# Five pairs of split weight buffers instead of four in a macaron trunk kernel, with silu, gate product and final norm done in place and the convolution's input projection wholly in split weights

## The chip, the cores and the metric

One core of one Trainium2 chip runs the whole program. The metric is the device time of one execution in microseconds (us). TensorE (PE) does the matmuls, VectorE (DVE) and ScalarE (ACT) the elementwise work, GpSimd (POOL) a few additions, and SyncE (SP) issues the weight transfers.

## The reference, cut to what matters

A trunk of two layers on x of 256 rows and 1024 columns, all in float32. Every layer adds half a gated feed-forward block, a mixer, and half a second feed-forward block. The mixer of layer 0 is a pair of convolutions, that of layer 1 is attention.

```
def swiglu_ffn(x, w_gate_up, w_down):
    gate, up = jnp.split(x @ w_gate_up, 2, axis=-1)
    return (jax.nn.silu(gate) * up) @ w_down

def conv_mixers(h, w_in, a_kernel, b_kernel, b_bias, b_ln_g, b_ln_b, w_out):
    z = h @ w_in
    a_b, a_c, a_x, b_val, b_gate = jnp.split(z, [...], axis=-1)
    y_a = a_b * causal_depthwise_conv(a_c * a_x, a_kernel)
    u = b_val * jax.nn.sigmoid(b_gate)
    u = causal_depthwise_conv(u, b_kernel) + b_bias.astype(u.dtype)
    y_b = jax.nn.silu(layer_norm(u, b_ln_g, b_ln_b))
    return jnp.concatenate([y_a, y_b], axis=-1) @ w_out

for layer in range(DEPTH):
    x = x + 0.5 * swiglu_ffn(rms_norm(x, ffn1_norm[layer]), ...)
    x = x + mixer(rms_norm(x, mix_norm[layer]))
    x = x + 0.5 * swiglu_ffn(rms_norm(x, ffn2_norm[layer]), ...)
return rms_norm(x, final_norm)
```

`D_FF` is 2816; `a_kernel` has 3 taps and `b_kernel` 31, on 512 channels each.

## The kernel before, in words

**Layout.** x lies in SBUF as eight tiles of 128 columns by 256 rows (`x[:, 0]` to `x[:, 7]`). The gain of a norm is put on x before a projection and the factor r of each row after it (`twice(r)`), so that a projection may start before r is known.

**Weights.** The weights come as a stream of units of 1 MB, each 128 by 2048 numbers or 16 tiles of 128 by 128, in the order of use. `load` (L111) brings a unit into one of four `raw` buffers. `split` (L117) makes two parts from it: ACT rounds it into `w1` (L126), DVE subtracts, `w2 = raw - w1` (L127), each in halves of 128x1024, or in quarters for the units in `FINE`. There are `WS` = 4 pairs of `w1` and `w2`. A raw buffer comes free when its unit has been split, a pair when PE has used it. `advance(u, n)` (L130) asks for loads up to unit `u + RAWS + WS - 1` and for splits up to `u + n`; the program calls it once per unit. Units in `whole` are not split: PE reads them from their raw buffer.

**Matmuls.** With a split unit and a split operand, `mm2` (L166) does two matmuls for each weight tile, one of 512 columns (L168) and one of 256 (L169). `mm3` (L158) does three of 256 columns (L162 to L164), and for a whole unit a single float32 one (L160), which the trace records as two.

**Stages.** Feed-forward (`ffn`, L364): 22 units for gate and up (p from 0 to 21) fill PSUM banks of the tag `pa`, of which there are four. `project2` (L324) takes two banks for a p, `project` (L314) one; the first stage takes one for p of 1 to 3 and also for the first p, whose unit is whole (L352). `join` (L334) or a product (L381) makes v from the banks, ACT makes the silu (L385), DVE the gate product (L387), and `split_to` (L183) splits the product. Then 22 units for down (L392), whose sums DVE adds to x (L404) tile by tile; with each tile `after.add` splits the next stage's operand (`xs`, L189 and L190) and sums its squares.

**Convolution stage** (`conv`, L422). Its 14 units are counted from `first_conv`: 0 to 9 for ten projections (p), 10 to 13 for the output projection. `WHOLE` names those that stay whole: 2 and 9, whose operand is `xg` (L428, eight activations), and 10 to 13. Projections 0 to 3 give u (L498 to L500), 4 to 7 give the short convolution `ya` (L513 to L522), 8 and 9 its gate (L532, L533). The 31 taps are shared: DVE does some (L463, sums in PSUM), while ACT makes products (`prod`, L485, 18 buffers) that POOL adds one after the other into `yp` (L486, 55 additions). L472 joins the two in y. Then the output projection on `ya` (`out_half`, first half) runs while the layer norm of y is worked out (L555 to L571); its result `ob` feeds the second half, and DVE adds the sums to x (L419). `AHEAD[p]` is how far `advance` may split at projection p, `PER_STEP` and `PER_POOL` how many taps are put behind it.

**What sets the order.** Each engine runs its instructions in program order. That order is set by a scheduler, from the order of the code, `tc.high_priority` and the `advance` calls; a wait on one engine holds all that stands behind it there.

Of the kernel before, what the change touches and what calls it, by code (L numbers as in the profile page):

```python
# [10 lines left out]
F32 = mybir.dt.float32  # L11
F32R = mybir.dt.float32r
I32 = mybir.dt.int32
AF = mybir.ActivationFunctionType
# [3 lines left out]
P = 128  # L18
D = 1024
S = 256  # L20
DEPTH = 2
FF = 2816
ND = D // P
# [10 lines left out]
UT = 16  # L34
# [2 lines left out]
POOL_TAPS = [13, 17, 13, 16]  # L37
PER_STEP = [9, 8, 7, 8, 8, 8, 9, 8, 9, 10]
PRIO = 0
WHOLE = {2, 9, 10, 11, 12, 13}  # L40
PBUFS = 18
PER_POOL = [6, 8, 2, 6, 6, 9, 6, 4, 8, 9]
XPRIO = 0
AHEAD = [2, 4, 1, 1, 4, 4, 3, 4, 3, 3]
LATE = 15
OUT_AHEAD = [2, 3]
PRIO_LN = 800
# [18 lines left out]
M_POOL = [0, 0, 0, 0]  # L66
B_POOL = [0, 0]
RAWS = 4
WS = 4
TWO = (3,)  # L70
ROBIN = False
SU_POOL = 2
# [21 lines left out]
def trunk(ctx: ExitStack, tc: tile.TileContext, xin, wst, cst, bia, idn, out):  # L94
    nc = tc.nc
# [5 lines left out]
    tmp = ctx.enter_context(tc.tile_pool(name="tmp", bufs=2))  # L101
# [70 lines left out]
    x = keep.tile([P, ND, S], F32, name="x")  # L172
    xs_all = keep.tile([P, ND * 2 * S + LINE // 4], F32R, name="xs")
    const_all = keep.tile([P, LINE // 4], F32, name="const")
    const = const_all[:, :NCONST]
# [17 lines left out]
    def rsqrt_of(sums, n, eps, eps_tile=None):  # L193

        ts = [slice(t, t + 1) for t in range(2)]
        with tc.high_priority(offset=0 if eps_tile is not None else PRIO_C):
            pt = psb.tile([P, 2, 2], F32, name="pb")
            for i, part in enumerate(sums):
                for t in range(2):
                    nc.tensor.matmul(pt[:, t, :], part[:, t * P:(t + 1) * P], ones[:, :2],  # L200
                                     start=i == 0 and t == 0, stop=i == len(sums) - 1,
                                     skip_group_check=True)
            a = tmp.tile([P, 2], F32, name="ra")
            y = tmp.tile([P, 2], F32, name="ry")
            q = tmp.tile([P, 2], F32, name="rq")
            if eps_tile is None:
                for t, c in enumerate(ts):
                    nc.vector.tensor_scalar(q[:, c], pt[:, t, :1], 1.0 / n, eps,
                                            op0=ALU.mult, op1=ALU.add)
                for c in ts:  # L210
                    nc.vector.tensor_scalar(y[:, c].bitcast(I32), q[:, c].bitcast(I32), 1, None,
                                            op0=ALU.logical_shift_right)
                for t, c in enumerate(ts):
                    nc.vector.tensor_scalar(a[:, c], pt[:, t, :1], -0.5 / n, -0.5 * eps,
                                            op0=ALU.mult, op1=ALU.add)
                for c in ts:
                    nc.vector.tensor_scalar(y[:, c].bitcast(I32), y[:, c].bitcast(I32), -1,
                                            0x5F3759DF, op0=ALU.mult, op1=ALU.add)
            else:
                nc.scalar.activation(y, pt[:, :, 0], AF.Sqrt, scale=1.0 / n, bias=eps_tile)  # L220
                nc.vector.tensor_scalar(a, pt[:, :, 0], -0.5 / n, -0.5 * eps,
                                        op0=ALU.mult, op1=ALU.add)
                for c in ts:
                    nc.vector.reciprocal(y[:, c], y[:, c])
            n = 3 if eps_tile is None else 1
            for i in range(n):
                for c in ts:
                    nc.vector.scalar_tensor_tensor(q[:, c], y[:, c], a[:, c], y[:, c],
                                                   op0=ALU.mult, op1=ALU.mult)
                for c in ts:  # L230
                    nc.vector.scalar_tensor_tensor(q[:, c] if i == n - 1 else y[:, c], q[:, c],
                                                   0.5 if i == n - 1 else 1.5, y[:, c],
                                                   op0=ALU.add, op1=ALU.mult)
            for c in ts:
                nc.vector.tensor_add(y[:, c], y[:, c], q[:, c])
            wide = tmp.tile([P, 2, P], F32, name="wide")
            pr = psb.tile([P, S], F32, name="pb")
            for t, c in enumerate(ts):
                nc.vector.tensor_copy(wide[:, t], y[:, c].to_broadcast([P, P]))
                nc.tensor.matmul(pr[:, t * P:(t + 1) * P], wide[:, t], ident,  # L240
                                 start=True, stop=True)
        return y, pr
# [68 lines left out]
    def twice(r):  # L311
        return r[:, None, :].to_broadcast([P, 2, S])

    def project(st, base, xs, xg=None):  # L314

        bank = psa.tile([P, 2, S], F32, name="pa")
        for i in range(2):
            for k in range(ND):
                w = st.tile(base + 2 * k + i)
                b = (xs[:, k, 0], xs[:, k, 1]) if len(w) == 2 else (xg[:, k],)  # L320
                mm3(bank[:, i], w, b, k == 0, k == ND - 1)
        return bank

    def project2(st, base, xs):  # L324
# [39 lines left out]
    def ffn(norm, after, between=None, first=None):  # L364
        _, r = norm.end(True, first is None)
        with tc.tile_pool(name="gp", bufs=1, reuse_waits="tile") as gp:
            st = take(NF)
# [3 lines left out]
            for p in range(NF):  # L371
                advance(st.u + p)
                one = p < ONES[st.u // FFN_STEP] or p >= NF - ONE_END
                if one:
                    bank = first if first and p == 0 else project(st, p * UT, norm.xs)
                else:
                    banks = project2(st, p * UT, norm.xs)
                with tc.high_priority(offset=PRIO_F):
                    v = tmp.tile([P, 2, S], F32, name="v")
                    if one:  # L380
                        nc.vector.tensor_mul(v, bank, twice(r))  # L381
                    else:
                        join(v, banks, r)
                    sl = tmp.tile([P, S], F32, name="sl")
                    nc.scalar.activation(sl, v[:, 0], AF.Silu)  # L385
                    g = tmp.tile([P, S], F32, name="g")
                    nc.vector.tensor_mul(g, sl, v[:, 1])  # L387
                    split_to(gs[:, p, 0], gs[:, p, 1], g)
            if between:
                between(gs[:, NF - 1, 0, :1].bitcast(F32))  # L390
            st = take(NF * ND // UT)
# [30 lines left out]
    def conv(norm, after):  # L422
        with tc.tile_pool(name="cp", bufs=1, reuse_waits="tile") as cp, \
                tc.tile_pool(name="cp2", bufs=PBUFS, reuse_waits="tile") as cp2:
            xg = cp.tile([P, ND, S], F32, name="xg")
            with tc.high_priority(offset=XPRIO):
                for k in range(ND):
                    nc.scalar.activation(xg[:, k], x[:, k], AF.Copy,  # L428
                                         scale=const[:, norm.col + k:norm.col + k + 1])
            _, r = norm.end(WIDEC)  # L430
            ob = cp.tile([P, 4, S], F32, name="ob")
            u = cp.tile([P, 4, KB - 1 + S], F32, name="u")
# [57 lines left out]
            st = take(10)  # L490
            for p in range(10):
                advance(st.u + p, AHEAD[p])
                bank = project(st, p * UT, norm.xs, xg)
                c = p % 4
                with tc.high_priority(offset=PRIO):
                    if p < 4:
# [6 lines left out]
                        queue_v += new[:LATE] + [f for f in [held_last] if f] + new[LATE:]  # L503
                        queue_p += [(c, f) for f in taps_p(c)]
                    elif p < 8:
                        t = tmp.tile([P, S], F32, name="g")
                        mc = m[:, c, KA - 1:]
                        if M_POOL[c]:
                            nc.scalar.copy(t, bank[:, 0])
# [211 lines left out]
            ffn(norm, nxt)  # L721
            norm = nxt
    with tc.tile_pool(name="fp", bufs=1, reuse_waits="tile") as fp:
        y = fp.tile([P, ND, S], F32, name="y")
        eps = fp.tile([P, 1], F32, name="eps")
        warm = fp.tile([P, 1], F32, name="warm")
        nc.vector.memset(eps, RMS_EPS)
# [98 lines left out]
```

## Time and profile before

| | |
|---|---|
| median of 3 runs | 960.96 us (960.74 to 962.14) |
| the profiled execution | 960.66 us, span 958.9 us |
| granted TensorE clock | 0.997 of full speed |
| PE busy | 945.5 us, 99% of the span |
| DVE busy | 724.3 us, 76% |
| ACT busy | 543.3 us, 57% |
| POOL busy | 47.1 us, 5% |
| mean DMA rate | 184 GB/s |

All times in the rows are counted from the start of the span. "Busy" for PE is from the start of a matmul to its modelled end, and matmuls overlap; the pace is therefore read from starts. "Idle before" in a row is the engine's idle time just before it, and the arrow names what ended it. The 2.1 us between the execution and its span lie around the program.

### The profile page before, as it was taken

Reading aid. Unit: us, or ns where it says so; the run is one execution under the profiler, and the core shown is the slowest. Engines: PE = TensorE matmul, PEld = TensorE weight load, DVE = VectorE, ACT = ScalarE, POOL = GpSimd, SP = SyncE. Lnnn points to the kernel's source line nnn. Section 1 sums busy time; section 2 is a strip of 40 time slices with the busy share of each in tenths; the row PEclk is TensorE's granted clock in tenths of the full one; section 3 lists DMA queues with packets and bytes.
Section 4 is the critical chain, followed back from the end, with each engine's and each line's share of the span. In section 5 each row is a group of like instructions: output and inputs, shape, how many; then the busy total and the mean of one; then the engine's idle time right before and its main releaser. Section 6 shows DMA issues by size and latency. Waiting matters only on the chain.

```text
span 958.9 us, 15090 instructions
## 1 busy us (share of the span) xinstructions
PE 945.5 (99%) x5828; PEld 845.8 (88%) x5828; DVE 724.3 (76%) x1373; ACT 543.3 (57%) x975; POOL 47.1 (5%) x61
## 2 busy tenths in 40 slices
PE   8999999999999999999999999999999999999996
PEld 7988898999888888988988889898888998889886
DVE  7988866688879878766788877665698798788552
ACT  6666554488265565554466565444676565665541
POOL 0000000049600000000000000000000000000000
PEclk9999999999999999999999999999999999999998
DMA  8855555544176555555455555555553455555501
GB/s 328 291 205 192 178 206 189 178 159 148 45 260 213 193 207 181 180 211 181 176 194 202 176 191 205 178 195 212 195 191 129 149 186 194 194 202 177 194 26 44
DMA packets 27287, 176.24 MB, mean 184 GB/s; under 512 B 3024, under 2 KB 3792, under 8 KB 6864
## 3 DMA queue, kind: packets, MB, share of 16 engines
q1 hardware_dynamic: 26784, 174.67, 51.7%
q8 instruction: 45, 0.74, 0.3%
q10 hardware_dynamic: 432, 0.63, 0.2%
q14 instruction: 26, 0.21, 0.1%
HBM read 174.23 MB, written 1.05 MB: 183 GB/s over the span
## 4 chain that ended last, share of the span: by engine, by line
PE 90%; POOL 3%; DVE 3%; ACT 1%; DMA 1%; issue 1%; SPq 0%; DVEq 0%; POOLq 0%; ACTq 0%
PE pa L168 33%; PE pa L169 17%; PE pb L168 15%; PE pb L169 8%; PE pa L162 4%; PE pa L163 3%; PE pa L164 3%; POOL yp L486 3%; PE pa L160 2%; PE pb L162 1%; PE pb L163 1%; PE pb L164 1%; DVE pb L463 1%; PE pa L352 1%; PE pb L652 1%
## 5 line engine op out<-in xcount | busy, mean ns | idle before, releaser
L127 DVE TENSOR_TENSOR w<-raw,w 128x1024 fp32r<-128x1024 f32 (+1 forms) x316 | 377.0, 1205 | 136.3 <-ACT w L126 135.9
L168 PE MATMUL pa<-xs,w 128*128 128x512 f32 x1376 | 479.4, 391 | 0.1
L126 ACT CAST w<-raw 128x1024 fp32r<-128x1024 f32 (+1 forms) x316 | 320.5, 1032 | 133.5 <-PE pa L168 49.7
L169 PE MATMUL pa<-xs,w 128*128 128x256 f32 x1376 | 387.2, 282 | 0.0
L168 PEld LDWEIGHTS pa<-xs,w 128*128 128x128 f32 x1376 | 258.1, 188 | 54.9 <-DVE xs L190 0.7
L169 PEld LDWEIGHTS pa<-xs,w 128*128 128x128 f32 x1376 | 260.0, 189 | 0.3
L168 PE MATMUL pb<-gs,w 128*128 128x512 f32 x616 | 213.7, 390 | 0.0
L169 PE MATMUL pb<-gs,w 128*128 128x256 f32 x616 | 173.7, 282 | 0.0
L168 PEld LDWEIGHTS pb<-gs,w 128*128 128x128 f32 x616 | 115.6, 188 | 24.1
L169 PEld LDWEIGHTS pb<-gs,w 128*128 128x128 f32 x616 | 116.4, 189 | 0.0
L385 ACT ACTIVATE sl<-v 128x256 f32<-128x256 f32 x88 | 36.8, 418 | 108.7 <-DVE v L340 104.3
L338 ACT COPY sq<-pa 128x256 f32<-128x256 f32 x172 | 62.9, 366 | 28.6 <-PE pa L169 26.1
L163 PE MATMUL pa<-xs,w 128*128 128x256 f32 x272 | 76.3, 281 | 0.1
L162 PE MATMUL pa<-xs,w 128*128 128x256 f32 x272 | 76.3, 282 | 0.0
L164 PE MATMUL pa<-xs,w 128*128 128x256 f32 x272 | 76.2, 281 | 0.0
L339 DVE TENSOR_TENSOR v<-pa,sq 128x256 f32<-128x256 f32 x156 | 65.5, 420 | 0.0
L404 DVE SCALAR_TENSOR_TENSOR x<-pb,x 128x256 f32<-128x256 f32 x60 | 25.4, 423 | 42.5 <-PE pb L169 28.5
L189 ACT ACTIVATE xs<-x,const 128x256 fp32r<-128x256 f32 x48 | 24.3, 506 | 55.2 <-DVE x L404 43.1
L486 POOL TENSOR_TENSOR yp<-yp,prod 128x256 f32<-128x256 f32 x55 | 45.1, 822 | 208.8 <-ACT prod L485 204.8
L340 DVE TENSOR_TENSOR v<-v,rr 128x512 f32<-128x512 f32 x78 | 53.6, 688 | 0.0
L162 PEld LDWEIGHTS pa<-xs,w 128*128 128x128 f32 x272 | 51.4, 190 | 0.3
L163 PEld LDWEIGHTS pa<-xs,w 128*128 128x128 f32 x272 | 51.1, 188 | 0.5 <-DVE xs L190 0.3
(155 smaller groups left out, 900.7 us busy)
## 6 DMA issues: line engine op xcount, KB each, us to landing
raw<-wst SPq DMA_DIRECT2D x159, 1024.0 KB, 4.8
bt<-bia SPq DMA_DIRECT2D x8, 384.0 KB, 3.3
raw<-wst SPq DMA_DIRECT2D x7, 256.0 KB, 6.3
raw<-wst SPq DMA_DIRECT2D x2, 512.0 KB, 5.6
x<-xin SPq DMA_DIRECT2D x3, 256.0 KB, 5.7
out<-y SPq DMA_DIRECT2D x2, 256.0 KB, 2.5
out<-y ACTq DMA_DIRECT2D x2, 256.0 KB, 2.4
x<-xin SPq DMA_DIRECT2D x2, 128.0 KB, 3.2
```

The source lines that it names most:

```text
L126: nc.scalar.copy(w1[u][:, c], raw[u][:, c])
L127: nc.vector.tensor_sub(w2[u][:, c], raw[u][:, c], w1[u][:, c].bitcast(F32))
L162: nc.tensor.matmul(o, a[0], b[0], start=start, stop=False, skip_group_check=check)
L163: nc.tensor.matmul(o, a[0], b[1], start=False, stop=False, skip_group_check=check)
L164: nc.tensor.matmul(o, a[1], b[0], start=False, stop=stop, skip_group_check=check)
L168: nc.tensor.matmul(o, w[0], b, start=start, stop=False, skip_group_check=True)
L169: nc.tensor.matmul(o[:, 0], w[1], b[:, 0], start=False, stop=stop, skip_group_check=True)
L338: nc.scalar.copy(h, bank[:, 1])
L339: nc.vector.tensor_add(v[:, i], bank[:, 0], h)
L340: nc.vector.tensor_mul(v, v, twice(r))
L385: nc.scalar.activation(sl, v[:, 0], AF.Silu)
L486: nc.gpsimd.tensor_add(yp[:, c], yp[:, c], t)
```

## The change

The number of pairs `WS` becomes 5, and with it both the standard lead of the splits (5) and that of the loads (8). Room for the fifth pair is made in several places. The silu and the gate product are written over v instead of into tiles of their own; the final norm's `y` is x itself; `xg` and its eight activations are gone, the convolution's temporary takes the buffers of `rw`, and `wide` has one buffer. Units 2 and 9 of the convolution stage are now split like the others, and `AHEAD` has new numbers.

```diff
-WHOLE = {2, 9, 10, 11, 12, 13}
+WHOLE = {10, 11, 12, 13}
...
-XPRIO = 0
-AHEAD = [2, 4, 1, 1, 4, 4, 3, 4, 3, 3]
+AHEAD = [4, 4, 3, 3, 4, 4, 4, 3, 2, 1]
...
-WS = 4
+WS = 5
...
-            wide = tmp.tile([P, 2, P], F32, name="wide")
+            wide = tmp.tile([P, 2, P], F32, name="wide", bufs=1)
...
-    def project(st, base, xs, xg=None):
+    def project(st, base, xs):
...
-                w = st.tile(base + 2 * k + i)
-                b = (xs[:, k, 0], xs[:, k, 1]) if len(w) == 2 else (xg[:, k],)
-                mm3(bank[:, i], w, b, k == 0, k == ND - 1)
+                mm3(bank[:, i], st.tile(base + 2 * k + i), (xs[:, k, 0], xs[:, k, 1]), k == 0,
+                    k == ND - 1)
...
-                    sl = tmp.tile([P, S], F32, name="sl")
-                    nc.scalar.activation(sl, v[:, 0], AF.Silu)
-                    g = tmp.tile([P, S], F32, name="g")
-                    nc.vector.tensor_mul(g, sl, v[:, 1])
-                    split_to(gs[:, p, 0], gs[:, p, 1], g)
+                    nc.scalar.activation(v[:, 0], v[:, 0], AF.Silu)
+                    nc.vector.tensor_mul(v[:, 1], v[:, 0], v[:, 1])
+                    split_to(gs[:, p, 0], gs[:, p, 1], v[:, 1])
...
-            xg = cp.tile([P, ND, S], F32, name="xg")
-            with tc.high_priority(offset=XPRIO):
-                for k in range(ND):
-                    nc.scalar.activation(xg[:, k], x[:, k], AF.Copy,
-                                         scale=const[:, norm.col + k:norm.col + k + 1])
...
-                bank = project(st, p * UT, norm.xs, xg)
+                bank = project(st, p * UT, norm.xs)
...
-                        t = tmp.tile([P, S], F32, name="g")
+                        t = tmp.tile([P, S], F32, name="rw")
...
-        y = fp.tile([P, ND, S], F32, name="y")
+        y = x
```

With the removed lines the numbers shift: L127 is L126 afterwards, L126 is L125, L160 is L159, L381 is L379, L387 is L383, L415 stands for L419, L454 for L463, L508 for L517, L513 for L522, L523 and L524 for L532 and L533.

The order of the work moves in three places. The first is DVE at the start of the first feed-forward stage, from the product for p = 0 to that for p = 1; `w` written from `raw` is a half of a unit's split. Before:

```order
L381 TENSOR_TENSOR v<-pa,rr 128x512
L127 TENSOR_TENSOR w_254<-raw,w_253 128x1024
L387 TENSOR_TENSOR g<-sl,v 128x256
L127 TENSOR_TENSOR w_254<-raw,w_253 128x1024
L381 TENSOR_TENSOR v<-pa,rr 128x512
L187 TENSOR_TENSOR gs<-g,gs 128x256
```

After:

```order
L379 TENSOR_TENSOR v<-pa,rr 128x512
L126 TENSOR_TENSOR w_246<-raw,w_245 128x1024 x2
L383 TENSOR_TENSOR v<-v 128x256
L126 TENSOR_TENSOR w_260<-raw,w_259 128x1024 x2
L186 TENSOR_TENSOR gs<-v,gs 128x256
L379 TENSOR_TENSOR v<-pa,rr 128x512
```

Four halves instead of two, and one more small operation, now stand between the two products.

The second is DVE in the convolution stage, around the second group of the short convolution (p = 5), whose first instruction (L522, afterwards L513) waits for an activation. `w_2532` is the split of unit 9, which had none before. Before:

```order
L514 TENSOR_TENSOR m<-pa,g 128x256
L463 SCALAR_TENSOR_TENSOR pb<-u,const,pb 128x256
L513 TENSOR_TENSOR g<-pa,rsq 128x256
L522 SCALAR_TENSOR_TENSOR pa<-m,const,pa 128x256
L463 SCALAR_TENSOR_TENSOR pb<-u,const,pb 128x256
L522 SCALAR_TENSOR_TENSOR ya<-m,const,pa 128x256
L463 SCALAR_TENSOR_TENSOR pb<-u,const,pb 128x256
L514 TENSOR_TENSOR m<-pa,g 128x256
```

After:

```order
L505 TENSOR_TENSOR m<-pa,rw 128x256
L454 SCALAR_TENSOR_TENSOR pb<-u,const,pb 128x256
L126 TENSOR_TENSOR w_2532<-raw,w_2531 128x1024
L513 SCALAR_TENSOR_TENSOR pa<-m,const,pa 128x256
L454 SCALAR_TENSOR_TENSOR pb<-u,const,pb 128x256
L513 SCALAR_TENSOR_TENSOR ya<-m,const,pa 128x256
L454 SCALAR_TENSOR_TENSOR pb<-u,const,pb 128x256
L126 TENSOR_TENSOR w_2532<-raw,w_2531 128x1024
L454 SCALAR_TENSOR_TENSOR pb<-u,const,pb 128x256
L504 TENSOR_TENSOR rw<-pa,rsq 128x256
L454 SCALAR_TENSOR_TENSOR pb<-u,const,pb 128x256
L505 TENSOR_TENSOR m<-pa,rw 128x256
```

From that L522 to the first L533 there were 35 instructions; from that L513 to the first L524 there are 37, the second half of unit 9's split and one L504 more. Of the 55 products on ACT all stood ahead of the second L517; now 54 stand ahead of the second L508. On PE, seven matmuls on `ya` stood ahead of the layer norm's first matmul (L557), and now four.

The third is DVE at the start of the second feed-forward stage of layer 0, at the addition of the fourth x tile (L419, afterwards L415; the first three stand above). `w_2981` is the split of the third unit of that stage, `w_2966` the same afterwards. Before:

```order
L127 TENSOR_TENSOR w_2935<-raw,w_2934 128x1024 x2
L190 SCALAR_TENSOR_TENSOR xs<-x,const,xs 128x256
L299 TENSOR_TENSOR sums<-sums,sq 128x256
L190 SCALAR_TENSOR_TENSOR xs<-x,const,xs 128x256
L299 TENSOR_TENSOR sums<-sums,sq 128x256
L419 TENSOR_TENSOR x<-pa,x 128x256
L127 TENSOR_TENSOR w_2981<-raw,w_2980 128x1024
```

After:

```order
L126 TENSOR_TENSOR w_2960<-raw,w_2959 128x1024 x2
L189 SCALAR_TENSOR_TENSOR xs<-x,const,xs 128x256
L298 TENSOR_TENSOR sums<-sums,sq 128x256
L189 SCALAR_TENSOR_TENSOR xs<-x,const,xs 128x256
L126 TENSOR_TENSOR w_2966<-raw,w_2965 128x1024 x2
L298 TENSOR_TENSOR sums<-sums,sq 128x256
L415 TENSOR_TENSOR x<-pa,x 128x256 x3
```

The whole split of that unit now stands ahead of the fourth tile. From the split of the stage's second unit to the row factor's first Newton step there were five halves, and there are nine.

## Rows read from the trace of the kernel before

**Rows 1.** The page's busy time and share of each engine, over the whole span.

```profile
PE 945.5 (99%) x5828; PEld 845.8 (88%) x5828; DVE 724.3 (76%) x1373; ACT 543.3 (57%) x975; POOL 47.1 (5%) x61
```

**Rows 2.** Timeline of PE, conv stage: start us, us, operation, count, idle before.

```profile
245.82 0.28 PE L164 MATMUL pa<-xs,w 128*128 128x256 f32 x1
...
246.29 7.07 PE L160 MATMUL pa<-xg,raw 128*128 128x256 f32 x32
254.87 3.29 PE L160 MATMUL pa<-ya,raw 128*128 128x256 f32 x14 [1.50 <-DVE ya L533]
257.99 0.59 PE L557 MATMUL pb<-sums,ones 128*128 128x256 f32 x2
...
270.28 10.52 PE L160 MATMUL pa<-ob,raw 128*128 128x256 f32 x48
280.45 0.58 PE L168 MATMUL pa<-xs,w 128*128 128x512 f32 x1
```

**Rows 3.** Timeline of DVE, conv stage: the wait, and the first half of ya.

```profile
240.76 0.49 DVE L522 SCALAR_TENSOR_TENSOR pa<-m,const,pa 128x256 f32<-128x256 f32 x1 [4.27 <-ACT pa L517]
...
254.09 0.72 DVE L533 TENSOR_TENSOR ya<-ya,v 128x512 f32<-128x512 f32 x1
```

**Rows 4.** Timeline of ACT, conv stage: the last product.

```profile
239.85 0.51 ACT L485 ACTIVATE prod<-u,const 128x256 f32<-128x256 f32 x1 [0.30 <-POOL yp L486]
```

**Rows 5.** The chain that ended last, two of POOL's additions: start us, us.

```profile
206.00 0.73 POOL yp L486
...
223.55 1.60 POOL yp L486
```

**Rows 6.** Timeline of DVE: a half of a split beside that second addition.

```profile
223.18 1.37 DVE L127 TENSOR_TENSOR w<-raw,w 128x1024 fp32r<-128x1024 f32 x1
224.47 0.48 DVE L463 SCALAR_TENSOR_TENSOR pb<-u,const,pb 128x256 f32<-128x256 f32 x1
```

**Rows 7.** Timeline of DVE, start of the first feed-forward stage.

```profile
27.09 1.22 DVE L127 TENSOR_TENSOR w<-raw,w 128x1024 fp32r<-128x1024 f32 x1
28.22 0.42 DVE L387 TENSOR_TENSOR g<-sl,v 128x256 f32<-128x256 f32 x1
28.55 1.22 DVE L127 TENSOR_TENSOR w<-raw,w 128x1024 fp32r<-128x1024 f32 x1
29.69 0.68 DVE L381 TENSOR_TENSOR v<-pa,rr 128x512 f32<-128x512 f32 x1
...
37.10 0.69 DVE L381 TENSOR_TENSOR v<-pa,rr 128x512 f32<-128x512 f32 x1
...
40.30 0.42 DVE L339 TENSOR_TENSOR v<-pa,sq 128x256 f32<-128x256 f32 x1
```

**Rows 8.** Timeline of PE, same stage: the first matmuls into two banks.

```profile
39.76 0.39 PE L168 MATMUL pa<-xs,w 128*128 128x512 f32 x1
...
42.53 0.39 PE L168 MATMUL pa<-xs,w 128*128 128x512 f32 x1
```

**Rows 9.** Timeline of DVE, start of the second feed-forward stage.

```profile
280.22 0.42 DVE L419 TENSOR_TENSOR x<-pa,x 128x256 f32<-128x256 f32 x1
280.55 1.22 DVE L127 TENSOR_TENSOR w<-raw,w 128x1024 fp32r<-128x1024 f32 x1
...
299.86 0.69 DVE L340 TENSOR_TENSOR v<-v,rr 128x512 f32<-128x512 f32 x1
300.46 0.42 DVE L339 TENSOR_TENSOR v<-pa,sq 128x256 f32<-128x256 f32 x1
```

**Rows 10.** Timeline of PE, same stage: the fourth and the 49th weight tile.

```profile
281.69 1.03 PE L168 MATMUL pa<-xs,w 128*128 128x512 f32 x2
...
301.74 0.39 PE L168 MATMUL pa<-xs,w 128*128 128x512 f32 x1
```

**Rows 11.** Busy time by stretch: us, then PE, PEld, DVE, ACT, POOL, clock, DMA.

```profile
50.00:190.00 140.00, 140.00 (x840) 125.33 (x840) 103.25 (x158) 77.10 (x126) 0.00 (x0) 1.00 0.54 193
...
281.00:320.00 39.00, 38.82 (x220) 33.86 (x219) 36.26 (x78) 24.28 (x47) 0.00 (x0) 1.00 0.68 245
```

## The prediction

> **What bounds the kernel now.** I read the page first: PE is busy for 99% of the span and DVE for 76% [rows 1], so a microsecond moves the end only if PE gains or loses it. Then I looked at the time by stretch. In the steady feed-forward stretches PE has no idle time, while DVE is busy for 103 us of 140 [rows 11]. What the change adds to DVE there has a cover of 37 us in 140. Where a stage begins, DVE is nearly full: 36.26 us of 39.00 [rows 11]. The waits and PE's timeline show its longest pause after the start in the convolution stage: 1.50 us before the output projection, released by the first half of `ya` on DVE [rows 2]. That half ends a chain: POOL's additions free the buffers of ACT's products (0.30 us idle before the last one, released by POOL [rows 4]); the activation behind the last product holds DVE for 4.27 us; then DVE works without a gap until `ya` is there [rows 3]. So that stage's end is set by POOL, ACT and DVE. The granted clock is 1.00, the upper level (2.4 GHz), in all these stretches [rows 11]; a pause as short as these did not lower it.
>
> **The change, part by part.**
>
> *Two units split instead of whole.* A float32 matmul takes (280.45 - 270.28)/24 = 0.424 us [rows 2], a unit of 16 takes 6.78. Split, it is 48 matmuls at (246.29 - 245.82)/4 = 0.1175 us [rows 2], or 5.64. PE gains 1.14 us per unit and 2.3 us for units 2 and 9. Before, it stood idle from 254.87 - 1.50 = 253.37; now it comes to the output projection at about 251.1. This is worth something only if `ya` is there earlier too.
>
> *The convolution's chain.* (a) One product fewer stands ahead of the activation that releases DVE: -0.81 us, the 0.30 idle and 0.51 busy of a product that waits for POOL [rows 4]. (b) Unit 9 now has a split, and its first half stands just ahead of the waiting instruction, beside POOL's additions. An addition takes 0.73 us alone and 1.60 beside such a half [rows 5, 6]: +0.87. (c) The chain may begin a little earlier, as eight activations for `xg` are gone from ACT and a matmul's turn on PE moves; but a half of a split now stands ahead of the row factor's first step on DVE. I take -0.2, between 0 and -0.5. The release of DVE thus stays at 240.76 - 0.81 + 0.87 - 0.2 = 240.6. (d) From there DVE needed 254.09 + 0.72 - 240.76 = 14.05 us [rows 3] for 35 instructions; now there are 37. The second half of unit 9 costs 1.13 us (28.22 - 27.09 [rows 7]) to 1.29 (224.47 - 223.18, beside POOL [rows 6]), and the L504 about 0.33 (pitch of a 128x256 operation, 28.55 - 28.22 [rows 7]): 15.6 in all. `ya` is there at 256.2 instead of 254.8: +1.4, and PE waits some 5 us instead of 1.5. (e) The layer norm's first matmul, at 257.99 before [rows 2], follows `ya` through the same seven DVE instructions as before, so it also comes 1.4 later; but only four `ya` matmuls instead of seven stand ahead of it, and the other three are left for later: 3 x 0.424 = +1.3. The stage ends 2.7 us later. Bounds: 1.0 (the half beside POOL falls into a gap, the start is 0.5 earlier) to 3.8 (the first half meets two additions, as one half took 1.37 us [rows 6] and an addition 0.73).
>
> The trace shows what such a meeting costs: the half ran from 223.18 to 224.47, the addition from 223.55 to 225.15 [rows 5, 6], which is the rest of the half and then 0.73. The Trainium skill ("SBUF — State Buffer", section "Who interferes with whom") says that a VectorE instruction with two SBUF inputs and a GpSimd one that reads SBUF exclude each other for the whole instruction, so that the later one waits for all of what is left of the other. By that rule an addition that starts right behind a half would lose 1.3 instead of 0.87, and the forecast would be 0.4 us higher, as only the first half meets POOL ahead of DVE's release; the row's own 0.87 is taken in the sum.
>
> *Five pairs at the start.* DVE is full there, and two more halves and a small operation stand between the products for p = 0 and p = 1: the second moves from 29.69 to 29.69 + 2 x 1.13 + 0.33 = 32.28 [rows 7]. Counting the operations on (halves 1.13, small ones 0.33, products 0.60, that is 300.46 - 299.86 [rows 9]) the product for p = 3 starts at 39.34 instead of 37.10 and the first join at 42.87 instead of 40.30 [rows 7]. PE wants the bank of the first at 39.76 and that of the second at 42.53 [rows 8]. The product ends at 39.34 + 0.69 = 40.03: PE loses 0.33 with 0.06 for the handover, as from 254.81 to 254.87 in [rows 2, 3]. The join ends at 43.29; PE would come at 42.86 and loses 0.49. Sum +0.8, bounds 0.2 to 1.5. Before, these places cost nothing; the cover was 2 us wide and the delay is larger.
>
> *Five pairs after the whole units.* At the start of the second feed-forward stage DVE now does both halves of the third unit ahead of the fourth x tile: 280.22 + 2.26 + 0.42 = 282.9 [rows 9]. That addition frees the bank which PE's fourth weight tile writes, at 281.69 before, where PE already lost about 0.5 (two matmuls in 1.03 us [rows 10]). It now loses 1.3, net +0.8, on top of the shift of the whole stage. Four more halves stand ahead of the row factor: 4.5 us, of which up to 2.7 go into idle time (39.00 - 36.26 [rows 11]), while a half and the first product (1.73) now stand behind the next join. That join starts between 300.46 + 4.5 - 2.7 - 1.73 = 300.5 and 303.2, takes 0.42, and PE wants its bank at 301.74 + 0.8 = 302.5 [rows 9, 10]. The wait is 0 to 1.2; I take 0.3. Sum +1.1, bounds 0 to 2.3.
>
> *The rest, at nothing.* The silu and the product in place have the same shapes; v is held until its product is split, but on DVE that split already stands ahead of the next join but one. The four casts and four halves more lie in the chain above or beside PE. The final norm in place has the same activations. One more load ahead on SP waits for a raw buffer as its predecessor did, since the split that frees it is also one unit earlier; the bias loads queued behind it keep their lead. `wide` is never needed twice at once. If v's longer hold did bind, it would cost 22 times per stage; I see no place for it.
>
> The sum is 2.7 + 0.8 + 1.1 = +4.6 on the profiled 960.66 us, or **965.3 us**. The median of the runs is 960.96, 0.3 above the profiled execution, and I leave the 0.3 in the range.
>
> **The rivals.** (1) *PE's gain comes through.* If DVE's release depends less on POOL than its position on ACT says, because the chain starts earlier and the extra half falls into the 4.27 us in which DVE waits [rows 3], `ya` is ready when PE comes. Then the 2.3 us and the pause of 1.5 are gained, and the start costs at most 0.8: 960.66 - 3.8 + 0.8 = 957.7, or less with the later stage unchanged. It decides in this direction once the release comes before about 235.5 (251.1 minus 15.6), 5 us earlier. For it: DVE has idle time in front of the release, and five pairs put splits ahead of the stage. Against: all but one product still stand ahead of the release, each waiting for POOL, and the splits of units 6 to 9 stay inside POOL's window. (2) *Nothing to measure.* The lead of five pairs is limited by the four raw buffers except at the two starts, and the waits there are half of my count: conv +1.0, others +0.4: 962, inside 0.2% of the time, which is about 1.9 us and what a measurement of this kernel can tell from no change. For it: most PE pauses before are below 0.5 us. (3) *Slower still.* Both starts at their upper bounds, and each of POOL's meetings at its worst: 960.66 + 3.8 + 1.5 + 2.3 = 968.3. For it: DVE has 2.7 us spare in 39 [rows 11].
>
> **How the numbers follow.** The forecast with its neighbours between 963 and 967.5 has 0.49, rival (1) 0.26, rival (2) 0.20, rival (3) 0.05. The slower cases are the forecast and (3), 0.54. The range goes from rival (1)'s time, rounded down, to just short of (3): 957.5 to 967.5; it leaves out some cases of (1) with a larger gain and most of (3). The forecast's own range is 962.5 to 967.5.
>
> **What would show it.** Right: PE's pause before the first matmul on `ya` is 4 to 6 us, released by L524; DVE's wait at the second L513 ends at 240 to 241; POOL's last addition ends at 255 to 256; there are pauses of about 0.3 and 0.5 us near 40 and 43, and one above 1 us near 284. Wrong: `ya` before 253, or no new pause in the first 50 us. A gain above 2 us means that the chain through POOL was not what sets that stage; then the release of DVE in the changed trace says which wait fell.

## The result, and the profile after

The changed kernel takes 968.77 us (median of 4 runs, 967.60 to 969.42); in the same comparison the kernel before takes 960.85. The ratio is 1.0072, with a 95% interval of 1.0058 to 1.0086: 0.7% slower. The forecast was 965.3 us, slower, with 957.5 to 967.5 as its range. The direction was right, and the time lies 1.3 us above the range.

Three marks that both traces have show where the time went: the first matmul of the first down projection, the first of the second feed-forward stage, and the first of that stage's down projection.

| stretch, us of the profiled execution | before | after | difference | forecast |
|---|---|---|---|---|
| span's start to the first down projection | 131.33 | 132.32 | +1.0 | +0.8 |
| from there to the second feed-forward stage (the convolution stage lies here) | 149.12 | 153.28 | +4.2 | +2.7 |
| from there to its down projection (the restart) | 126.73 | 129.39 | +2.7 | +1.1 |
| from there to the last down projection | 480.49 | 480.43 | -0.1 | 0 |

The spans are 958.9 and 966.6 us, so 1.8 us of the execution lay around the program before (not 2.1), and 1.9 lie there after. So the three places of the forecast hold the whole loss, and the steady stretches do not change. Two places cost clearly more than was counted, by 1.5 and 1.6 us.

What PE waited for, in the profile after (us in total, times, longest us):

```profile
PE pa L159 <- DVE ya L524: 6.2, 1, 6.2
PE pb L239 <- DVE wide L238: 1.6, 1, 1.6
PE pa L167 <- DVE x L415: 1.4, 1, 1.4
PE pa L350 <- DVE xg L346: 1.3, 1, 1.3
PE pa L167 <- DVE v L337: 1.2, 2, 0.9
...
PE pa L167 <- DVE v L379: 0.2, 1, 0.2
```

The 1.5 us in front of the output projection [rows 2] have become 6.2. The fourth x tile (L415), the joins (L337) and the product for p = 3 (L379) are new waits, all at the places named in the forecast.

**The first stage.** The products for p = 1 and p = 3 and the first join on DVE, and the two banks on PE (timelines: start us, us):

```profile
32.23 0.68 DVE L379 TENSOR_TENSOR v<-pa,rr 128x512 f32<-128x512 f32 x1
...
39.31 0.68 DVE L379 TENSOR_TENSOR v<-pa,rr 128x512 f32<-128x512 f32 x1
42.85 0.42 DVE L337 TENSOR_TENSOR v<-pa,sq 128x256 f32<-128x256 f32 x1
```

```profile
40.05 0.51 PE L167 MATMUL pa<-xs,w 128*128 128x512 f32 x1 [0.19 <-DVE v L379]
43.41 0.47 PE L167 MATMUL pa<-xs,w 128*128 128x512 f32 x1 [0.32 <-DVE v L337]
```

These were at 29.69, 37.10 and 40.30 on DVE [rows 7] and at 39.76 and 42.53 on PE [rows 8]. Forecast were 32.28, 39.34 and 42.87. PE loses 43.41 - 42.53 = 0.9 us by the second bank.

**The convolution stage.** DVE from its release to `ya`, and ACT and POOL beside it:

```profile
237.48 1.61 DVE L126 TENSOR_TENSOR w<-raw,w 128x1024 fp32r<-128x1024 f32 x1
241.45 0.49 DVE L513 SCALAR_TENSOR_TENSOR pa<-m,const,pa 128x256 f32<-128x256 f32 x1 [2.36 <-ACT pa L508]
...
256.25 1.15 DVE L524 TENSOR_TENSOR ya<-ya,v 128x512 f32<-128x512 f32 x1
...
260.21 0.42 DVE L546 TENSOR_TENSOR sums<-sums,y 128x256 f32<-128x256 f32 x1
```

```profile
240.54 0.51 ACT L476 ACTIVATE prod<-u,const 128x256 f32<-128x256 f32 x1 [0.30 <-POOL yp L477]
240.95 0.46 ACT L508 ACTIVATE pa<-m,const 128x256 f32<-128x256 f32 x1
```

The chain that ended last, POOL's addition beside the first half of unit 9's split and the one behind it (start us, us):

```profile
238.09 1.60 POOL yp L477
...
239.76 0.75 POOL yp L477
```

All of POOL's additions, and what follows them (timeline):

```profile
205.73 51.12 POOL L477 TENSOR_TENSOR yp<-yp,prod 128x256 f32<-128x256 f32 x55 [205.29 <-ACT prod L476]
256.81 1.17 POOL L546 TENSOR_TENSOR sums<-y 128x256 f32<-128x256 f32 x1
```

The release comes at 241.45; less the 0.99 by which the whole stage starts later that is 240.46, and 240.6 was forecast. The addition that meets unit 9's half takes 1.60 us, as counted. From the release to `ya` it takes 256.25 + 1.15 - 241.45 = 15.95 us against 15.6: the last product (L524) took 1.15 instead of 0.72 [rows 3]. It began at 256.25, and POOL's last addition beside it ended at 205.73 + 51.12 = 256.85. The Trainium skill ("SBUF — State Buffer", section "Who interferes with whom") lets either of the two that comes second wait for the other; here it is VectorE that came second and took 0.43 us longer, which the forecast had priced for the halves of a split and not for this product, and the trace agrees with the page.

PE behind that pause, and the granted clock by stretch (us, then busy PE, PEld, DVE, ACT, POOL, clock, DMA share, GB/s):

```profile
257.45 3.78 PE L159 MATMUL pa<-ya,raw 128*128 128x256 f32 x8 [6.18 <-DVE ya L524]
261.03 1.06 PE L548 MATMUL pb<-sums,ones 128*128 128x256 f32 x2
261.88 3.25 PE L159 MATMUL pa<-ya,raw 128*128 128x256 f32 x14
265.34 0.61 PE L199 MATMUL pb<-ones,sums 128*128 128x2 f32 x4 [0.21 <-DVE sums L558]
```

```profile
251.00:257.00 6.00, 0.27 (x3) 0.07 (x1) 6.00 (x15) 1.96 (x3) 5.45 (x9) 0.85 0.00 0
257.00:261.00 4.00, 3.55 (x8) 2.81 (x9) 3.50 (x8) 0.00 (x0) 2.02 (x2) 0.50 0.00 0
261.00:262.00 1.00, 1.00 (x4) 0.79 (x3) 0.00 (x0) 0.00 (x0) 0.00 (x0) 0.50 0.00 0
262.00:270.00 8.00, 7.79 (x40) 6.56 (x39) 5.95 (x34) 1.89 (x5) 0.00 (x0) 1.00 0.10 15
```

Here is what the forecast did not have: when PE goes on after 6.2 us, its clock is at 0.50, the lower level of 1.2 GHz, for about 4.5 us. Four `ya` matmuls (eight records) take 3.58 us, some 0.9 each, where seven took 3.12 before [rows 2]. Before, the clock stayed at 1.00 behind the pause of 1.50 us:

```profile
255.00:260.00 5.00, 5.00 (x24) 4.32 (x25) 4.11 (x12) 0.92 (x3) 1.12 (x2) 1.00 0.44 184
```

**The restart.** The fourth x tile and the first join of p = 1 on DVE, and one wait between them:

```profile
287.89 1.08 DVE L415 TENSOR_TENSOR x<-pa,x 128x256 f32<-128x256 f32 x3
...
299.33 1.23 DVE L126 TENSOR_TENSOR w<-raw,w 128x1024 fp32r<-128x1024 f32 x1 [0.98 <-ACT w L125]
...
308.91 0.41 DVE L337 TENSOR_TENSOR v<-pa,sq 128x256 f32<-128x256 f32 x1
```

```profile
298.24 1.05 ACT L125 CAST w<-raw 128x1024 fp32r<-128x1024 f32 x1 [1.64 <-PE pa L167]
```

On PE, the fourth weight tile and the bank of that join:

```profile
288.36 0.50 PE L167 MATMUL pa<-xs,w 128*128 128x512 f32 x1 [1.37 <-DVE x L415]
...
309.47 0.47 PE L167 MATMUL pa<-xs,w 128*128 128x512 f32 x1 [0.91 <-DVE v L337]
```

Counted from the stage's first matmul (280.45 before, 285.60 after) the join moved from 20.01 [rows 9] to 23.31 us, 3.3 later; the forecast had 0 to 2.7. The cast at 298.24 had to wait until PE let a pair go, and the split behind it stands on DVE ahead of the row factor's steps. DVE's busy time from the stage's first matmul to that join, before and after (us, then PE, PEld, DVE, ACT, POOL, clock, DMA share, GB/s):

```profile
280.45:300.46 20.01, 19.83 (x109) 17.05 (x108) 18.59 (x48) 11.71 (x22) 0.00 (x0) 1.00 0.64 247
285.60:308.91 23.31, 21.57 (x116) 18.11 (x114) 21.60 (x51) 14.15 (x25) 0.00 (x0) 1.00 0.79 305
```

DVE was idle for 1.42 us before and for 1.71 after: none of the four halves more went into idle time. On PE's weight loads (PEld) two short waits more stand between the fourth tile and that join, one for the row factor's sums and one for the second join of p = 0:

```profile
299.64 0.19 PEld L250 LDWEIGHTS pb<-sq,ones 128*128 128x128 f32 x1 [0.25 <-ACT sq L185]
...
302.74 0.19 PEld L167 LDWEIGHTS pa<-xs,w 128*128 128x128 f32 x1 [0.34 <-DVE v L337]
```

Matched weight tile by weight tile (with the two matmuls on the row factor's sums counted alike), PE had lost 1.0 us of the 2.7 when it came to the first of these waits, 1.5 behind the second, and 2.7 behind the bank of the next join.

### The profile page after: what moved, and what is told of

It is laid out like the page before. It is cut to its first block, busy times and chain, and to the rows that moved or that the text cites. A ratio compares the mean times of both kernels' runs of the same rounds, so it can differ in the third digit from the quotient of the medians.

```text
span 966.6 us, 15180 instructions
## 1 busy us (share of the span) xinstructions
PE 946.4 (98%) x5860; PEld 847.1 (88%) x5860; DVE 729.3 (75%) x1377; ACT 544.6 (56%) x971; POOL 49.5 (5%) x61
## 4 chain that ended last, share of the span: by engine, by line
PE 86%; DVE 6%; ACT 3%; DMA 2%; issue 1%; POOL 1%; SPq 0%; DVEq 0%; POOLq 0%; ACTq 0%
PE pa L167 31%; PE pa L168 16%; PE pb L167 14%; PE pb L168 8%; PE pa L161 3%; PE pa L162 3%; PE pa L163 3%; DVE w L126 2%; ACT prod L476 1%; DMA raw<-wst 1%; ACT w L125 1%; PE pb L162 1%; PE pb L161 1%; PE pb L163 1%; PE pa L159 1%; DVE pb L454 1%
## 5 line engine op out<-in xcount | busy, mean ns | idle before, releaser
L126 DVE TENSOR_TENSOR w<-raw,w 128x1024 fp32r<-128x1024 f32 (+1 forms) x320 | 381.9, 1206 | 137.5 <-ACT w L125 137.0
L125 ACT CAST w<-raw 128x1024 fp32r<-128x1024 f32 (+1 forms) x320 | 324.5, 1032 | 134.7 <-PE pa L167 51.6
L168 PE MATMUL pa<-xs,w 128*128 128x256 f32 x1376 | 387.2, 282 | 0.0
L167 PEld LDWEIGHTS pa<-xs,w 128*128 128x128 f32 x1376 | 258.1, 188 | 58.6 <-DVE x L415 1.7
L168 PEld LDWEIGHTS pa<-xs,w 128*128 128x128 f32 x1376 | 260.0, 189 | 0.3
L382 ACT ACTIVATE v<-v 128x256 f32<-128x256 f32 x88 | 36.8, 419 | 104.3 <-DVE v L338 100.7
L162 PE MATMUL pa<-xs,w 128*128 128x256 f32 x304 | 85.3, 281 | 0.1
L163 PE MATMUL pa<-xs,w 128*128 128x256 f32 x304 | 85.1, 280 | 0.0
L161 PE MATMUL pa<-xs,w 128*128 128x256 f32 x304 | 85.1, 281 | 0.0
L337 DVE TENSOR_TENSOR v<-pa,sq 128x256 f32<-128x256 f32 x156 | 64.8, 416 | 0.0
L163 PEld LDWEIGHTS pa<-xs,w 128*128 128x128 f32 x304 | 57.7, 190 | 0.2 <-DVE w L126 0.2
L477 POOL TENSOR_TENSOR yp<-yp,prod 128x256 f32<-128x256 f32 x55 | 47.1, 859 | 209.3 <-ACT prod L476 205.3
L162 PEld LDWEIGHTS pa<-xs,w 128*128 128x128 f32 x304 | 57.1, 188 | 0.4 <-DVE xs L189 0.3
L161 PEld LDWEIGHTS pa<-xs,w 128*128 128x128 f32 x304 | 57.0, 188 | 0.3
```

The costliest lines, as they stand in the source:

```text
L125: nc.scalar.copy(w1[u][:, c], raw[u][:, c])
L126: nc.vector.tensor_sub(w2[u][:, c], raw[u][:, c], w1[u][:, c].bitcast(F32))
L161: nc.tensor.matmul(o, a[0], b[0], start=start, stop=False, skip_group_check=check)
L162: nc.tensor.matmul(o, a[0], b[1], start=False, stop=False, skip_group_check=check)
L163: nc.tensor.matmul(o, a[1], b[0], start=False, stop=stop, skip_group_check=check)
L167: nc.tensor.matmul(o, w[0], b, start=start, stop=False, skip_group_check=True)
```

## The experiments

Theory A is that of the forecast: three places, two from the lead of five pairs, one from DVE's chain to `ya`. Theory B puts the loss on the buffers and the edits in place, theory C the missing part of the convolution stage on the clock. The stretches are those of the first table; the first one also holds the waits for the first transfers, which vary by some tenths. In two runs (34 products, 14 taps on POOL) it is about 2 us longer; in them the granted clock was 0.72 on average from 8 to 14 us, behind waits of PE of 2.27 and 2.17 us, where all others had 1.00. Each ratio is to runs of the kernel before on the same chip in the same hour, whose medians were 960.85 to 961.43. The stretches are of one profiled execution each.

| run | median us | ratio to before, 95% interval | start | convolution | restart | rest |
|---|---|---|---|---|---|---|
| before | 960.85 | | 131.33 | 149.12 | 126.73 | 480.49 |
| the change | 968.77 | 1.0072 (1.0058 to 1.0086) | 132.32 | 153.28 | 129.39 | 480.43 |
| four pairs | 967.02 | 1.0062 (1.0048 to 1.0075) | 131.12 | 155.65 | 126.59 | 480.50 |
| lead of four | 964.26 | 1.0030 (1.0018 to 1.0042) | 130.97 | 154.20 | 126.56 | 480.39 |
| in place only | 961.29 | 1.0001 (0.9992 to 1.0009) | 130.87 | 149.18 | 126.58 | 480.50 |
| in place, 22 products | 960.21 | 0.9994 (0.9986 to 1.0003) | 131.46 | 148.58 | 126.70 | 480.50 |
| 22 matmuls in the pause | 965.98 | 1.0041 (1.0026 to 1.0056) | 131.96 | 151.16 | 129.04 | 480.40 |
| 8 matmuls in the pause | 969.19 | 1.0072 (1.0055 to 1.0088) | 132.39 | 154.17 | 128.96 | 480.42 |
| unit 9 split alone | 964.04 | 1.0024 (1.0013 to 1.0036) | 130.91 | 150.96 | 126.65 | 480.47 |
| unit 2 split alone | 964.46 | 1.0029 (1.0019 to 1.0039) | 131.01 | 152.70 | 126.61 | 480.51 |
| four pairs, 34 products | 965.89 | 1.0041 (1.0026 to 1.0056) | 133.40 | 156.00 | 126.62 | 480.50 |
| 14 taps on POOL | 958.44 | 0.9969 (0.9959 to 0.9980) | 132.93 | 147.13 | 126.50 | 480.46 |
| 15 taps on POOL | 959.07 | 0.9974 (0.9964 to 0.9984) | 130.98 | 147.12 | 126.50 | 480.52 |

**Four pairs.**

```diff
-WS = 5
+WS = 4
```

> The changed kernel with WS = 4 again; everything else of the change stays, so units 2 and 9 of the convolution stage are still split. The two traces differ by 0.85 us up to the first down projection, by 4.3 more up to the first matmul of the second feed-forward stage, and by 2.6 more up to its down projection; all that follows is parallel. Theory A (the loss lies at these three places, and the first and the third come from the fifth pair's lead): the 0.85 and the 2.6 go, the 4.3 stay, so 960.85 + 4.3 = 965.2 us, between 964 and 966; PE's pause before the first matmul on ya stays at 5 to 6.5 us. Theory B (products and norm in place cost time, or the split of units 2 and 9 shifts the restart of the next stage by itself): 967 or more, with a pause above 1 us again at the fourth weight tile of that stage.

It took 967.02 us. Start and restart are back at the values of before, as theory A has it. The convolution stage, which should have stayed at 153.3, is 2.4 longer. With four pairs the order there is another one: all 55 products stand ahead of DVE's release, DVE waits 4.0 us for it instead of 2.36, and PE pauses 8.6 us, not the 5 to 6.5 that was expected. So the time lies above theory A's 966 and just at theory B's 967, but B's sign, a pause above 1 us at the fourth weight tile, is absent. The fifth pair is thus the cause at two places, and the third does not need it.

**Five pairs, lead of four.**

```diff
-    ahead_load, ahead_split = RAWS + WS - 1, WS
+    ahead_load, ahead_split = RAWS + WS - 1, 4
```

> The changed kernel with its five pairs of buffers, but advance splits only four units ahead (the loads stay eight ahead). Theory A (the order, that is the lead of five, costs the time): as with four pairs, 965.2 us, between 964 and 966.2; DVE's second product in the first stage is back near 29.7 us. Rival (the fifth pair itself costs time, by where its tiles lie or by loads that start earlier): near 968.8 us, above 967.5.

It took 964.26 us. The second product is at 29.34 us, and start and restart have no loss with five pairs in place. So it is the order that costs there, not the buffers. The rival is out. The remaining 3.4 us are the convolution stage's; the profiled execution, 1.4 us above the median, shows 5.1 there, behind a pause of 8.54 us.

**The edits in place alone.**

```diff
-                    nc.scalar.activation(sl, v[:, 0], AF.Silu)
-                    nc.vector.tensor_mul(g, sl, v[:, 1])
-                    split_to(gs[:, p, 0], gs[:, p, 1], g)
+                    nc.scalar.activation(v[:, 0], v[:, 0], AF.Silu)
+                    nc.vector.tensor_mul(v[:, 1], v[:, 0], v[:, 1])
+                    split_to(gs[:, p, 0], gs[:, p, 1], v[:, 1])
...
-        y = fp.tile([P, ND, S], F32, name="y")
+        y = x
```

The one buffer for `wide` and the convolution's temporary in `rw` belong to it too.

> The kernel before with the edits in place alone: silu and gate product in v, the final norm in x, the convolution's temporary in the buffers of rw, one buffer for wide. Four pairs, xg, WHOLE and AHEAD as before. Theory A (these edits cost nothing): 960.85 us, within 0.7 of it. Theory B (v is held longer, or the last norm waits in place): 1 us slower or more, spread over the 88 products or in the last 10 us.

The ratio is 1.0001 (0.9992 to 1.0009), and every stretch is that of before within 0.5 us. Theory B falls.

**22 and 8 matmuls in the pause**, on the changed kernel:

```diff
+            fill = psb.tile([P, S], F32, name="pb")
+            for _ in range(FILL):
+                nc.tensor.matmul(fill[:, :P], ones, ones, start=True, stop=True)
             out_half(st, accs, 0, [ya], range(8), OUT_AHEAD)
```

> The changed kernel with 22 matmuls of 128 columns on constants put on PE in front of the output projection, about 5.3 us of its 6.2 us pause; their result is not used. The order of PE moves too: eight ya matmuls instead of four now stand ahead of the layer norm's first matmul. The next run has that same order with eight such matmuls (1.9 us), so the two differ in the length of the pause alone. Theory C (the long pause lets the granted clock fall to half, and that is the part of the convolution stage's loss that the blind sum lacked): the clock stays at 1.00, the ya matmuls run at 0.42 us from the first, and the stage is 1.5 us (four matmuls fewer behind, little lost at the first matmul of the norm) plus 0.8 shorter: 966.5 us, between 965.8 and 967.3. Rival (the clock costs nothing here, as PE waits for the norm anyway): the same as the run with eight.

> As the run with 22 matmuls on constants, with eight: the same order, a pause of some 4.3 us in front of ya. Theory C: if a pause of 4.3 us lets the clock fall as 6.2 did, the eight ya matmuls take up to 0.85 us each and the norm's first matmul comes 1.5 to 2.5 us later than with 22: 968 to 969 us. If it does not, the same as with 22, which then says that the clock's fall needs a longer pause than 4.3 us. Rival (clock of no effect): both near 967.

PE with 22, and with 8 (timelines, then the stretch with the granted clock):

```profile
250.76 5.07 PE L544 MATMUL pb<-ones 128*128 128x128 f32 x44
257.12 3.72 PE L160 MATMUL pa<-ya,raw 128*128 128x256 f32 x16 [1.29 <-DVE ya L525]
260.68 0.59 PE L552 MATMUL pb<-sums,ones 128*128 128x256 f32 x2
...
257.00:261.00 4.00, 3.88 (x18) 3.44 (x19) 3.16 (x8) 0.00 (x0) 1.69 (x2) 1.00 0.00 0
```

```profile
251.21 1.95 PE L544 MATMUL pb<-ones 128*128 128x128 f32 x16
257.54 6.72 PE L160 MATMUL pa<-ya,raw 128*128 128x256 f32 x16 [4.39 <-DVE ya L525]
264.10 0.59 PE L552 MATMUL pb<-sums,ones 128*128 128x256 f32 x2
...
257.00:261.00 4.00, 3.46 (x8) 2.83 (x9) 3.58 (x8) 0.00 (x0) 2.11 (x2) 0.50 0.00 0
```

The same eight matmuls on `ya` take 3.56 us behind a pause of 1.29, and 6.56 behind one of 4.39, and the medians differ by 3.2 us: 965.98, inside the 965.8 to 967.3, and 969.19, just above the 968 to 969. The order is the same; only the number of matmuls on constants differs, and with it the pause. Theory C holds, and its price depends on how many matmuls stand ahead of the norm's first one: with eight it is 3.0 us. With the change's own four it can only be worked out: `sums` was done at 260.63 (L546 at 260.21, 0.42), the norm's matmul started at 261.03 and took 0.43 us longer than at full clock, together some 0.8 us, an estimate.

**One unit split at a time**, on the edits in place, with four pairs and the old `AHEAD`:

```diff
-WHOLE = {2, 9, 10, 11, 12, 13}
+WHOLE = {2, 10, 11, 12, 13}
```

> The edits in place alone on the kernel before, and unit 9 split, with four pairs and the old AHEAD; unit 2 stays whole with xg. Both halves of unit 9's split now stand on DVE between its release and ya, and the release stands behind 54 products instead of 55. Theory A (DVE's chain sets ya): release -0.8 us, ya +2.3 behind it, so ya 1.5 us later, a pause of about 4.1 us on PE although unit 9 takes PE 1.1 us less: 962.2 us if the clock holds, up to 964 if it falls. Rival (PE's own work sets the stage): 960.9 - 1.1 = 959.8.

The other has `{9, 10, 11, 12, 13}`.

> The edits in place alone on the kernel before, and unit 2 split, with four pairs and the old AHEAD; unit 9 stays whole with xg. DVE gets two more halves before POOL's last additions, and the second activation for the short convolution stays behind all 55 products. Theory A: two more additions take 1.60 instead of 0.73 if the halves fall beside POOL, release and ya up to 1.7 us later, pause on PE up to 4.3 us: 961 to 963 us. Rival (PE's own work sets the stage): 959.8.

Both are slower, 964.04 and 964.46, though each saves PE 1.1 us. With unit 9 split the release was 1.2 us earlier and `ya` 1.4 later than before; the profiled execution, at a mean clock of 0.997, kept its clock over a pause of 3.5 us and took 961.94, while nine others of the same kernel, at 0.992 to 0.996, took 963.7 to 965.9. What the clock did behind the pause in those nine no trace shows; a low mean alone does not place its fall, as the first stage can hold one too (14 taps on POOL: mean 0.994, with a fall between 8 and 14 us and none in the convolution stage). With unit 2 split POOL's additions ended at 255.9 instead of 254.2, the release came at 242.50, and behind a pause of 5.6 us the clock was 0.57 from 256 to 260. So neither unit's split pays in this stage, for the same reason: PE's saved time turns into pause, and DVE and POOL get the work. Expected were 962.2 to 964 and 961 to 963: the one is at its upper end, the other above it. Both runs have the old `AHEAD`; what its new numbers do by themselves was not tried.

**Buffers for the products.** In the room of the edits in place, on the kernel before:

```diff
-PBUFS = 18
+PBUFS = 22
```

> The edits in place alone on the kernel before, and the room they make given to the buffers of ACT's products: PBUFS 22 instead of 18. The order of the instructions is the same. The activation that releases DVE stands behind the last product, which then waits for POOL's addition 33 instead of 37. Theory A (products that wait for POOL hold DVE, and DVE's work from its release sets ya): release about 3.2 us earlier (4 x 0.81), near 237.5; ya ready near 251.6 to 252, PE does not wait for it (1.5 us gained at most), but the layer norm's first matmul is then held by POOL's last addition at 254.2: 959.4 us, between 959 and 960.3. Rival (POOL alone sets that stage): 960.9, no change.

DVE, then PE:

```profile
237.59 0.49 DVE L520 SCALAR_TENSOR_TENSOR pa<-m,const,pa 128x256 f32<-128x256 f32 x1 [1.00 <-ACT pa L515]
250.93 0.76 DVE L531 TENSOR_TENSOR ya<-ya,v 128x512 f32<-128x512 f32 x1
254.71 0.42 DVE L467 TENSOR_TENSOR yp<-yp,pb 128x256 f32<-128x256 f32 x1 [2.62 <-POOL yp L484]
```

```profile
253.32 2.75 PE L160 MATMUL pa<-ya,raw 128*128 128x256 f32 x12
257.05 0.70 PE L160 MATMUL pa<-ya,raw 128*128 128x256 f32 x2 [0.98 <-DVE ya L531]
```

The release is 3.2 us earlier and `ya` 3.1, as theory A says, and PE does not wait for it. Now POOL's last addition holds DVE for 2.62 us, and the second half of `ya` behind it holds PE. The interval of the ratio, 0.9986 to 1.0003, includes 1: the times do not show that 22 buffers alone gain anything.

With 34 product buffers on the run with four pairs (`PBUFS = 34`):

> The run with four pairs (967.0 us, units 2 and 9 split), with PBUFS 34 instead of 18 in the room of the fifth pair; the order of the instructions hardly moves. There DVE waited 4.0 us for its release, which stood behind products that wait for POOL. Theory A (that wait sets ya, POOL's last addition the norm): no wait at the release, ya some 4 us earlier in the stage, pause on PE near 4.5 us instead of 8.6, the norm's first matmul then held by POOL's last addition: 963 to 964.5 us. Rival (POOL alone sets the stage of the changed kernel): 967, no change.

The median is 965.89, above the 963 to 964.5. DVE no longer waited at its release, and `ya` came 4.1 us earlier in the stage; but PE still paused 6.78 us, the clock fell, and POOL's last addition held the norm until 262.67. The profiled execution, 969.46, was the slowest of four (964.8 to 966.7 the others), so its 156.0 us are no measure of the median.

**Taps from POOL to DVE**, on the run with 22 products:

```diff
-POOL_TAPS = [13, 17, 13, 16]
+POOL_TAPS = [13, 17, 13, 14]
```

> The run with edits in place and 22 product buffers (960.2 us) with two taps of the last channel moved from POOL to DVE (POOL_TAPS 13, 17, 13, 14). There DVE waited 2.6 us for POOL's last addition and PE 1.0 us for the second half of ya. Theory A: POOL ends about 1.6 us earlier, DVE's two taps (0.8) fit into its wait, PE's pause goes and the stage becomes PE's own: 1.0 us less, 959.2 us, between 958.7 and 960. Rival (DVE becomes the bound): 960.2 or more.

The other has 15 in the last place.

> The same with one tap moved (POOL_TAPS 13, 17, 13, 15). Theory A: POOL ends 0.8 us earlier, most of PE's pause of 1.0 goes: 959.5 us, between 959 and 960.2. Rival (DVE becomes the bound): 960.2 or more.

PE with 14, without a pause:

```profile
251.78 2.97 PE L160 MATMUL pa<-xg,raw 128*128 128x256 f32 x13
254.59 4.05 PE L160 MATMUL pa<-ya,raw 128*128 128x256 f32 x18
258.47 0.59 PE L555 MATMUL pb<-sums,ones 128*128 128x256 f32 x2
```

958.44 and 959.07 us, ratios 0.9969 (0.9959 to 0.9980) and 0.9974 (0.9964 to 0.9984). The first lies 0.3 us below the 958.7 to 960 expected, the second inside its range. The convolution stage is 2.0 us shorter than before in both, and PE sets it. Both beat the kernel before and the changed one. The taps moved with the old 18 buffers were not tried, so the gain is that of both edits together.

## Why the prediction was right, and where it was not

- **Direction and places: right.** All of the loss lies at the three places, and the steady stretches and the edits in place cost nothing, each shown by a run.
- **The start (+0.8): right**, 0.9 by the second bank, 1.0 by the stretch, with what the first transfers vary.
- **DVE's release (240.6) and the 37 instructions behind it: right** within 0.4 us. Of the part's items, the product fewer, the addition of 1.60 and the second half of unit 9 are as counted. What 14.05 could not show was the last product's 0.43 more beside POOL. POOL's last addition ended at 256.85, or 255.9 without the later start, inside the 255 to 256 expected.
- **The convolution stage (+2.7, bounds 1.0 to 3.8): the first failed step.** It measured +4.2. The forecast put the clock at nothing: the sentence that a pause as short as these did not lower it was read at 1.5 us (the two stretches of [rows 11] do not hold this stage, though the clock was 1.00 there too), and the forecast's own pause of 5 us was not priced. At 6.2 the clock fell to 0.50. Of the missing 1.5 us some 0.8 are the clock's by the working above; the rest is the stretched product and the layer norm's sums, which came some 0.3 us later behind `ya` (260.63 - 257.40 against 257.73 - 254.81), beside POOL. The forecast's bound came from DVE and POOL alone.
- **The restart (+1.1, bounds 0 to 2.3): the second failed step,** 2.7 measured. The wait for the fourth tile was right (1.37 in the profile, 1.3 forecast). The four halves ahead of the row factor were to go into idle time for up to 2.7 of 4.5 us. That idle time was read from a stretch that ends at 320; up to the join at 300.46 DVE had 1.42 us of it, and none was used up. Instead the split of the sixth unit waited itself, 0.98 us, for a pair that PE still held, so the join came 3.3 us later. The bank of that join cost PE 1.15 us where 0.3 was counted, and the two short waits before it, 0.5 us together, were not in the forecast. That the lead causes the loss, the run with a lead of four shows; the share of the one wait for a pair was not tried by itself.
- **The range.** Its upper end was set just short of rival (3), "both starts at their upper bounds", at 968.3 us with a chance of 0.05. Its time came, but not its mechanism: the start cost 1.0, not 1.5, POOL's meetings were as counted ahead of DVE's release, and the clock, which no rival had, did about half of the convolution stage's excess. The rival that PE's gain comes through, with 0.26, was refuted: the two units split alone were slower too.

## What to carry to other kernels

Where an engine's work is saved inside a stage that another chain ends, the saving becomes a pause; price the pause too, the clock behind it included, and not only the chain. A deeper lead of prefetched work cost time here where a stage starts, since it stands ahead of what the first results wait for, on an engine that runs in order, and gained nothing measurable in the steady stretches (480.4 to 480.5 us in every run). Whether a lead of five in the steady part alone would pay was not tried. In this kernel the freed memory paid as buffers between ACT and POOL together with one or two taps moved, and not as a fifth pair of weights.

## What was not expected of the hardware

The granted clock was at 0.50 behind pauses of PE of 4.39, 6.18, 6.78, 8.54 and 8.56 us, at 0.57 over the four microseconds that begin with the last of a 5.58 us pause, and at 1.00 behind one of 1.50 and, in one profiled execution, 3.47 us. With 22 matmuls whose result is not used put into the pause, 1.29 us of it were left and the clock was 1.00.

Near the start of the program it fell behind shorter waits: with 14 taps on POOL, PE waited 2.17 us before 9.04, and the clock was 0.72 on average from 8 to 14 us, where the kernel before, behind a wait of 1.91 us, had 1.00. The two stretches, 14 taps and before:

```profile
8.00:14.00 6.00, 4.96 (x15) 4.18 (x16) 5.29 (x16) 4.78 (x13) 0.00 (x0) 0.72 1.04 374
8.00:14.00 6.00, 5.38 (x25) 4.57 (x25) 6.00 (x18) 5.62 (x15) 0.00 (x0) 1.00 1.05 385
```

That profiled execution took 960.46 us, the longest of its eight, where the median is 958.44.
